# Three one-pass products in place of one wide product in a latent-attention stage, with the softmax division on another engine

## The chip, the cores and the metric

The kernel runs on one core of a Trainium2 chip. A core has five engines with instruction queues of their own: TensorE (PE in the profile; its weight loads stand apart as PEld) multiplies, VectorE (DVE) and ScalarE (ACT) work element by element, GpSimd (POOL) does slower side work, and SyncE (SP) mostly starts DMA transfers. Each engine takes its instructions in a fixed order and waits on semaphores for the others. The metric is the device time of one execution in microseconds (us); lower is better.

## What is computed

The reference is a decoder trunk of two layers on 256 positions of width 2048. Layer A (gated spatial mixing with attention into 256 memory tokens) and both gated feed-forward networks (FFN, with a causal convolution of width 3) are not changed. What matters is layer B, multi-head latent attention with 12 heads:

```python
q = (rmsnorm(q_lat, g_q_lat) @ w_uq).reshape(B, S, 12, 128 + 64)      # q_nope, q_rope
s = (einsum('bqhr,bkr->bhqk', einsum('bqhn,rhn->bqhr', q_nope, w_uk), c_kv)
     + einsum('bqhp,bkp->bhqk', q_rope, k_rope)) * (128 + 64) ** -0.5
p = softmax(where(k_pos <= q_pos, s, -inf))
o = einsum('bqhr,rhv->bqhv', einsum('bhqk,bkr->bqhr', p, c_kv), w_uv)  # 12 heads of 128
x = x + concat([o, memory_attention(q_m)]) @ w_out
x = x + conv_ffn(rmsnorm(x, g_ffn), w_up, cw, cb, w_down)
```

The end is a last rmsnorm. All data are f32.

## The kernel before

**Products in parts.** Activations lie transposed, 128 features by 256 positions in each block. A product with weights (512 KB, four column blocks by two row blocks, in one `chunk`) is made of parts: SP loads `raw` (four buffers), ScalarE rounds it to a high part `whi` in the reduced type fp32r (L110), VectorE subtracts to get the low part `wlo` (L111), four buffers each, and TensorE adds up high x high, high x low and low x high, one pass each. In `mm_fm` that is L147, L148 and L150; `gemm_fm` runs chunks in pairs through it, and its `hooks` are functions called after a numbered chunk. `gemm_tm` and `mm_tm` (L178 to L180) do the same with positions as rows. The activations are split in the same way (`split`, `split_pair`, `split_gain`).

**Small products** of the attention are plain f32, each of which the profile shows as two records. fp32r operands give one record.

**Layer B** first makes the latents `chl` (keys and values) and `qhl` (queries), the rotary key `krs`, already in parts, and the memory queries. Then a loop over six pairs of heads, `i`, runs: `queries(i)` and `keys(i)` (weight products, results copied out of PSUM to `qn` and `kn`); `turn` of the pair `i - 2` (three transposes, copy to `pT`, L889 and L891); in two rounds another third of the value columns by `values`, whose result v lies in the tile `scratch`; `scores` of the pair `i - 1`; `attend` of the pair `i - 2` (L898, L899); and one memory head's scores, turn and output in three successive rounds. Scores are causal: the first 128 queries meet 128 keys, the second 128 queries 256 keys, so a head's content score is one product of 128 moving columns and one of 256 (L865), to which two one-pass rotary products each are added (L867). The value products have the same two widths. In `scores`, VectorE masks and takes the maximum (L872), ScalarE the exponential with its sum (L877), VectorE the reciprocal (L880) and the multiplication by it (L882). The last turns and value products are hooks of the first group of `w_out`.

**Around it.** `w_out` adds to the residual (L554), prepares the FFN's operand (L242, L243) and, on GpSimd, its sum of squares (L268, L273). The FFN starts its first product at once and asks for the root of that sum in a hook: `rstd_bc` adds over the partitions by a product with ones (L262) and computes on VectorE and ScalarE the factors `rb`, first used when the first product's result is taken out (L228). In the last FFN the residual itself is turned from features to positions: four VectorE transposes (`turn` in `run`, L965) and 64 small DMAs on SP (`place`, L972), in hooks of the second and third round, needed when the down projection begins.

**Order.** Outside the first stage the order of each engine is not that of the code: the Tile library orders instructions by a simulated time line, so work that seems ready early can move ahead of code that stands before it, on each engine by itself. Buffers of a tag rotate; a new tile waits until the last reader of the old one is done. There are 8 PSUM banks, all of one tag.

Of the kernel before, what the change touches and what calls it, by code (L numbers as in the profile page):

```python
# [16 lines left out]
P = 128  # L17
# [54 lines left out]
class Kernel:  # L72
# [459 lines left out]
    def memory_turn(self, p, pool, bufs=2):  # L532
        nc = self.nc
        acc = self.psum()
        for mb in range(2):
            for sb in range(2):
                nc.tensor.transpose(
                    acc[:, mb * S + sb * P : mb * S + (sb + 1) * P], p[:, sb, mb * P : (mb + 1) * P], self.ident
                )
        pT = self.tmp(pool, [P, 512], "pT", bufs)  # L540
        nc.scalar.activation(pT, acc, AF.Copy)
        return pT

# [39 lines left out]
    def ffn(self, l, after=None, to_tokens=None, tokens=None):  # L583
        nc, t = self.nc, self.t
        rb = self.tmp(self.cp, [P, S], "rbc", 2)
        xhl, ssum = self.xhl, self.ssum
        first = {1: [lambda: self.rstd_bc(rb, ssum, D)]}
        up, down = t["w_ffn_up"][l], t["w_ffn_down"][l]
        with self.tc.tile_pool(name=self.uid("ff"), bufs=1) as fp:
            g0 = 0  # L590
            for part, ng in enumerate(FF_GROUPS):
                h = self.ap.tile([P, NB, 512], F32R, tag="big", name=self.uid("h"))

                def conv(b, acc):
                    a = self.tmp(fp, [P, 2, S], "a", 2)
                    self.scaled(a, acc, rb)
                    c = self.tmp(fp, [P, 2, S], "c", 3)
                    for i in range(2):
                        w = lambda j: self.cT[:, l, j, b + i : b + i + 1]
                        nc.scalar.activation(c[:, i, :], a[:, i, :], AF.Identity, scale=w(2), bias=w(3))  # L600
                        for j in (1, 0):
                            o = c[:, i, 2 - j :]
                            nc.vector.scalar_tensor_tensor(o, a[:, i, : S - 2 + j], w(j), o, ALU.mult, ALU.add)  # L603
                    return c

                for g in range(g0, g0 + ng):
                    gate = self.tmp(fp, [P, 4, S], "gate", 2)

                    def eg(b, acc):
                        c = conv(4 * g + b, acc)  # L610
                        nc.scalar.activation(gate[:, b : b + 2, :], c, AF.Silu)

                    def ev(b, acc):
                        c = conv(FB + 4 * g + b, acc)
                        hv = self.tmp(fp, [P, 2, S], "hv", 2)
                        nc.vector.tensor_tensor(hv, gate[:, b : b + 2, :], c, ALU.mult)
                        j = 4 * (g - g0) + b
                        self.split_pair(h[:, j : j + 2, :], hv)

                    ks = list(range(NB))  # L620
                    turns = to_tokens[g - 1] if to_tokens is not None and g in (1, 2) else {}
                    self.gemm_fm(self.rows(up, g * 512, 512), ks, 4, lambda k: xhl[:, k, :], eg, hooks=first if g == 0 else {})
                    self.gemm_fm(self.rows(up, FF + g * 512, 512), ks, 4, lambda k: xhl[:, k, :], ev, hooks=turns)
                last = part == len(FF_GROUPS) - 1
                if last and l == 0:
                    self.new_hl()
                dn = down[g0 * 512 : (g0 + ng) * 512]
                for j in range(4):
                    src = self.rows(dn, j * 512, 512)
                    if tokens is not None:  # L630
                        self.gemm_tm(
                            src, 4 * ng, 512, lambda k: h[:, k, :], lambda tb, acc: tokens(j, tb, acc, last), late=3 if last and j == 3 else 0
                        )
                        continue

                    def ed(b, acc):
                        self.add_residual(4 * j + b, acc)
                        if last:
                            after(4 * j + b)

                    self.gemm_fm(src, list(range(4 * ng)), 4, lambda k: h[:, k, :], ed)
                g0 += ng
# [92 lines left out]
    def layer_b(self):  # L735
# [9 lines left out]
        with tc.tile_pool(name="lb", bufs=1) as lb:  # L745
# [32 lines left out]
                return r  # L778

            ek, fk = latent("ck")  # L780
            self.gemm_fm(self.rows(wkv, 0, KR), ks, 4, x, ek, gain=gk, hooks={1: [lambda: self.rstd_bc(rb, ssum, D)]})
            eq, fq = latent("ql")
            self.gemm_fm(self.rows(w, 0, QR), ks, 4, x, eq, gain=gm, hooks={4: [lambda: fk(chl, KR, "g_kv_lat")]})

# [22 lines left out]
            self.gemm_fm(self.rows(w, QR, MW), ks, MH, x, em, gain=gm, hooks=hooks)  # L807

            hl = self.ap.tile([P, NB, 512], F32R, tag="big", name=self.uid("mainhl"))
            scratch = self.ap.tile([P, NB * 512], F32, tag="xhl", name="scratch")  # L810
            v = scratch[:, : 2 * GW].rearrange("p (a c) -> p a c", a=2)
            wuv = t["w_uv"][0].rearrange("r h v -> r (h v)")

            def values(c):
                def ev(tb, acc):
                    nc.scalar.activation(v[:, tb, c * 512 : (c + 1) * 512], acc, AF.Copy)

                self.gemm_tm(self.rows(wuv, c * 512, 512), 4, 512, lambda k: chl[:, k, :], ev)

# [6 lines left out]
            scale = HD ** -0.5  # L826
            qn, qr, kn, pa, pm = {}, {}, {}, {}, {}

            def queries(pr):
                banks = [self.psum() for _ in range(2)]  # L830
                accs = [banks[0][:, :S], banks[0][:, S:], banks[1][:, :S]]
                src = self.rows(wuq, pr * 2 * HD, 2 * HD)
                for c in range(0, 4, 2):
                    hi, lo = self.chunk(src(c, 2), 2, 2 * HD)
                    jobs = []
                    for j, a in enumerate(accs):
                        cols = slice(j * P, (j + 1) * P)
                        jobs += [(a, hi[:, i, cols], lo[:, i, cols], qhl[:, c + i, :], c + i == 0 and j != 1, c + i == 3 and j != 0) for i in range(2)]
                    self.mm_fm(jobs)
                qn[pr] = self.tmp(lp, [P, 2, S], "qn", 2)  # L840
                nc.scalar.activation(qn[pr], banks[0].rearrange("p (j s) -> p j s", j=2), AF.Copy)
                r = rotate(accs[2])
                qr[pr] = self.tmp(lp, [P, 2, S], "qr", 2, F32R)
                for j in range(2):
                    own, far = (slice(o * ROPE, (o + 1) * ROPE) for o in (j, 1 - j))
                    nc.scalar.activation(qr[pr][own, j, :], r[own, :], AF.Copy)
                    tt(qr[pr][far, j, :], r[own, :], qr[pr][own, j, :].bitcast(F32), ALU.subtract)

            def keys(pr):
                kn[pr] = self.tmp(lp, [P, 2, S], "kn", 2)  # L850

                def ev(b, acc):
                    nc.scalar.activation(kn[pr][:, b : b + 2, :], acc, AF.Copy)

                self.gemm_fm(self.rows(wuk, pr * 256, 256), list(range(4)), 2, lambda k: chl[:, k, :], ev, nk=4)

            def scores(h):
# [3 lines left out]
                for qb in range(2):  # L861
                    n = P * (qb + 1)
                    o = sc[:, part[qb]]
                    q = slice(qb * P, (qb + 1) * P)
                    mm(o, qn[pr][:, j, q], kn[pr][:, j, :n], start=True, stop=False)  # L865
                    for i in range(2):
                        mm(o, qr[pr][:, j, q], krs[:, i, :n], start=False, stop=i == 1)  # L867
                mx = self.tmp(lp, [P, 2], "mx", 4)
# [10 lines left out]
                    )  # L879
                nc.vector.reciprocal(den, den)  # L880
                for qb in range(2):
                    nc.vector.tensor_scalar(p[:, part[qb]], p[:, part[qb]], den[:, qb : qb + 1], None, ALU.mult)  # L882
                pa[h] = p

            def turn(h):
                p = pa.pop(h)
                acc = self.psum()
                for i in range(3):
                    nc.tensor.transpose(acc[:, i * P : (i + 1) * P], p[:, i * P : (i + 1) * P], self.ident)  # L889
                pT = self.tmp(lp, [P, 512], "pT", 3)  # L890
                nc.scalar.activation(pT[:, : 3 * P], acc[:, : 3 * P], AF.Copy)  # L891
                pa[h] = pT

            def attend(h):
                pT = pa.pop(h)
                o = self.psum()
                cols = slice(h * P, (h + 1) * P)
                mm(o[:, :S], v[:, 0, cols], pT[:, :S], start=True, stop=False)  # L898
                mm(o[:, P:S], v[:, 1, cols], pT[:, S : S + P], start=False, stop=True)  # L899
                self.split(hl[:, h, :], o[:, :S])  # L900

            def mscores(h):
                pm[h] = self.memory_scores(1, h, qm[:, h, :], lp)

            def mturn(h):
                pm[h] = self.memory_turn(pm[h], lp, 3)

            def mout(h):
                self.memory_out(1, h, pm.pop(h), hl)
# [29 lines left out]
    def run(self):  # L939
# [9 lines left out]
        with tc.tile_pool(name="fin", bufs=1) as fin:  # L949
# [11 lines left out]
            def turn(h):  # L961
                small[h] = self.tmp(fin, [P, 8, 2, 4, 32], "small", 1)
                for j in (0, 4):
                    src = self.x[:, 8 * h + j : 8 * h + j + 4, :].rearrange("p j s -> p (j s)")
                    nc.vector.transpose(small[h][:, j : j + 4].rearrange("p j a b c -> p (j a b c)"), src)  # L965

            def place(h, q):
                lanes = lambda i: slice(32 * i, 32 * i + 32)
# [116 lines left out]
```

## Time and profile before

| | us |
|---|---|
| median of 3 runs (2047.09 to 2047.97) | 2047.1 |
| the profiled execution | 2048.53 |
| its span, first to last instruction | 2046.8 |
| PSUM copies of L841 and L853 (ScalarE, 6 each), mean | 0.585 and 0.589 |
| copy of the turned p, L891 (12), mean | 0.486 |
| copy of the values, L816 (6), mean | 0.595 |
| loads of w_ffn_up, issue to landing, median | 4.2 |

"Busy" counts the time in which an engine has an instruction at work. Matmul records overlap in the pipeline, each longer than its share, so the cost of a product is read from the distance between the starts of successive records in a timeline. A timeline row gives start, duration, engine, line, operation, what is written from what, partitions and elements, and a count of merged records; in square brackets stands the idle time ahead and what ended it. A row of the waits gives the waiting line, what it waited for, the total, the number and the longest. A row of the table by stretches gives the stretch, its length, busy time with instructions of TensorE, its loads, VectorE, ScalarE and GpSimd, then the granted clock, the DMA share and the GB/s.

### The profile page before, as it was taken

How to read it: one execution, taken by the hardware profiler on the slowest of the kernel's cores; microseconds unless marked ns; L12 is line 12 of the kernel's file. 1: busy time of each engine (PE TensorE's matmuls, PEld its weight loads, DVE VectorE, ACT ScalarE, POOL GpSimd, SP SyncE). 2: the span in 40 equal slices, each digit the busy share in tenths (PEclk: the TensorE clock that was granted, in tenths of full speed). 3: DMA queues.
4: the chain of work that ended last, by engine and by line, in shares of the span. 5: the costliest groups of instructions: out<-in, count | busy, mean ns of one | idle time of the engine just before them, and what ended most of it. 6: DMA issues, size and time to landing. Idle time of an engine off the chain costs nothing.

```text
span 2046.8 us, 39055 instructions
## 1 busy us (share of the span) xinstructions
PE 2036.8 (100%) x16232; PEld 1970.7 (96%) x16232; DVE 1356.2 (66%) x1859; ACT 1044.0 (51%) x1345; POOL 94.2 (5%) x125
## 2 busy tenths in 40 slices
PE   9999999999999999999999999999999999999998
PEld 8989999999999999999999999999988999889997
DVE  6855667767556666457688875776655667656665
ACT  6754644555435554345555665455544455434553
POOL 0000013000000000000052001300000000000000
PEclk9999999999999999999999999999999999999999
DMA  8675565666656666566665545786666666666654
GB/s 309 192 225 176 155 197 187 197 196 188 204 187 194 196 194 197 188 196 195 187 196 181 174 129 176 198 224 196 195 195 193 190 198 193 194 195 188 196 185 155
DMA packets 220626, 394.62 MB, mean 193 GB/s; under 512 B 31648, under 2 KB 38176, under 8 KB 220320
## 3 DMA queue, kind: packets, MB, share of 16 engines
q1 hardware_dynamic: 220160, 391.60, 62.0%
q8 instruction: 127, 2.08, 0.4%
q10 hardware_dynamic: 288, 0.52, 0.1%
q14 instruction: 51, 0.42, 0.1%
HBM read 387.88 MB, written 2.10 MB: 191 GB/s over the span
## 4 chain that ended last, share of the span: by engine, by line
PE 99%; POOL 0%; DVE 0%; issue 0%; ACT 0%; POOLq 0%
PE ps L150 26%; PE ps L147 26%; PE ps L148 26%; PE ps L178 6%; PE ps L179 6%; PE ps L180 6%; PE ps L865 0%; PE ps L485 0%; PE ps L484 0%; PE ps L487 0%; PE ps L548 0%; PE ps L513 0%; PE ps L688 0%; PE ps L898 0%; PE ps L867 0%; PE ps L288 0%
## 5 line engine op out<-in xcount | busy, mean ns | idle before, releaser
L111 DVE TENSOR_TENSOR wlo<-raw,whi 128x1024 fp32r<-128x1024 f32 (+1 forms) x672 | 817.5, 1233 | 615.7 <-issue 419.0
L110 ACT ACTIVATE whi<-raw 128x1024 fp32r<-128x1024 f32 (+1 forms) x672 | 705.2, 1056 | 800.3 <-PE ps L148 571.7
L147 PE MATMUL ps<-xhl,whi 128*128 128x256 f32 x3264 | 752.1, 277 | 0.0
L148 PE MATMUL ps<-xhl,whi 128*128 128x256 f32 x3264 | 750.6, 276 | 0.0
L147 PEld LDWEIGHTS ps<-xhl,whi 128*128 128x128 f32 x3264 | 612.8, 188 | 0.3
L148 PEld LDWEIGHTS ps<-xhl,whi 128*128 128x128 f32 x3264 | 612.6, 188 | 0.3
L150 PE MATMUL ps<-xhl,wlo 128*128 128x256 f32 x3264 | 404.3, 276 | 0.0
L150 PEld LDWEIGHTS ps<-xhl,wlo 128*128 128x128 f32 x3264 | 385.6, 188 | 0.2
L147 PE MATMUL ps<-h,whi 128*128 128x256 f32 x704 | 161.6, 276 | 0.0
L148 PE MATMUL ps<-h,whi 128*128 128x256 f32 x704 | 161.5, 276 | 0.0
L603 DVE SCALAR_TENSOR_TENSOR c<-a,cT,c 128x255 f32<-128x255 f32 (+1 forms) x352 | 146.3, 479 | 0.0
L179 PE MATMUL ps<-wlo,h 128*128 128x512 f32 (+1 forms) x364 | 139.0, 382 | 0.0
L180 PE MATMUL ps<-whi,h 128*128 128x512 f32 (+1 forms) x364 | 138.7, 382 | 0.0
L178 PE MATMUL ps<-whi,h 128*128 128x512 f32 (+1 forms) x364 | 138.3, 382 | 0.0
L147 PEld LDWEIGHTS ps<-h,whi 128*128 128x128 f32 x704 | 132.0, 188 | 0.0
L148 PEld LDWEIGHTS ps<-h,whi 128*128 128x128 f32 x704 | 131.9, 188 | 0.0
L600 ACT ACTIVATE c<-a,cT 128x256 f32<-128x256 f32 x176 | 91.6, 591 | 73.9 <-DVE a L228 73.9
L147 PE MATMUL ps<-mainhl,whi 128*128 128x256 f32 x512 | 118.0, 277 | 0.0
L148 PE MATMUL ps<-mainhl,whi 128*128 128x256 f32 x512 | 117.9, 276 | 0.0
L147 PEld LDWEIGHTS ps<-mainhl,whi 128*128 128x128 f32 x512 | 96.1, 188 | 0.0
L148 PEld LDWEIGHTS ps<-mainhl,whi 128*128 128x128 f32 x512 | 96.1, 188 | 0.0
L150 PE MATMUL ps<-h,wlo 128*128 128x256 f32 x704 | 86.9, 276 | 0.0
(246 smaller groups left out, 1973.6 us busy)
## 6 DMA issues: line engine op xcount, KB each, us to landing
raw<-in_w_ffn_up SPq DMA_DIRECT2D x352, 512.0 KB, 4.2
raw<-in_w_ffn_down SPq DMA_DIRECT2D x176, 512.0 KB, 4.7
raw<-in_w_out SPq DMA_DIRECT2D x64, 512.0 KB, 4.8
raw<-in_w_in_a SPq DMA_DIRECT2D x56, 512.0 KB, 4.3
raw<-in_w_mem_kv SPq DMA_DIRECT2D x30, 512.0 KB, 5.2
raw<-in_w_in_b SPq DMA_DIRECT2D x16, 512.0 KB, 3.9
raw<-in_w_uq SPq DMA_DIRECT2D x12, 384.0 KB, 3.2
raw<-in_w_kv_a SPq DMA_DIRECT2D x8, 512.0 KB, 3.8
```

What stands on the lines that cost most here:

```text
L110: nc.scalar.activation(hi[:, :n], raw[:, :n], AF.Copy)
L111: nc.vector.tensor_tensor(lo[:, :n], raw[:, :n], hi[:, :n].bitcast(F32), ALU.subtract)
L147: mm(acc, wh, x[:, :S], start=first, stop=False)
L148: mm(acc, wh, x[:, S:], start=False, stop=False)
L150: mm(acc, wl, x[:, :S], start=False, stop=last)
L178: mm(acc, xh, wh, start=first, stop=False)
L179: mm(acc, xh, wl, start=False, stop=False)
L180: mm(acc, xl, wh, start=False, stop=last)
L600: nc.scalar.activation(c[:, i, :], a[:, i, :], AF.Identity, scale=w(2), bias=w(3))
L603: nc.vector.scalar_tensor_tensor(o, a[:, i, : S - 2 + j], w(j), o, ALU.mult, ALU.add)
```

## The change

- `queries` and `keys` keep high and low parts (`parts`: a copy on ScalarE, a subtraction on VectorE, both out of PSUM) in place of one f32 copy; `values` keeps two halves `vh`, `vl`; the turned p is split too.
- A content score is three one-pass products, high x high, high x low, low x high; so is each value product.
- The division by the softmax sum is a ScalarE copy with a scale.
- To make room: two buffers for the heads' `pT` (of 3), one for the turned memory scores of layer B (of 3 shared ones, under a tag `mT` of its own), and 2048 instead of 4096 bytes of DMA scratch, which lies at address 0 of SBUF, so everything moves by that much.
- `rstd_bc` is called after chunk 3 instead of 1 in both FFNs and at the latent keys.
- The residual's four transposes are pinned: each stays behind the instruction that the code has before it on VectorE.

```diff
-        first = {1: [lambda: self.rstd_bc(rb, ssum, D)]}
+        first = {3: [lambda: self.rstd_bc(rb, ssum, D)]}
...
-            scratch = self.ap.tile([P, NB * 512], F32, tag="xhl", name="scratch")
-            v = scratch[:, : 2 * GW].rearrange("p (a c) -> p a c", a=2)
+            scratch = self.ap.tile([P, NB * 512], F32R, tag="xhl", name="scratch")
+            vh, vl = (scratch[:, o * GW : (o + 2) * GW].rearrange("p (a c) -> p a c", a=2) for o in (0, 2))
...
-                    nc.scalar.activation(v[:, tb, c * 512 : (c + 1) * 512], acc, AF.Copy)
+                    hi, lo = (x[:, tb, c * 512 : (c + 1) * 512] for x in (vh, vl))
+                    nc.scalar.activation(hi, acc, AF.Copy)
+                    tt(lo, acc, hi.bitcast(F32), ALU.subtract)
...
+            def parts(hl, x):
+                nc.scalar.activation(hl[:, 0], x, AF.Copy)
+                tt(hl[:, 1], x, hl[:, 0].bitcast(F32), ALU.subtract)
...
-                qn[pr] = self.tmp(lp, [P, 2, S], "qn", 2)
-                nc.scalar.activation(qn[pr], banks[0].rearrange("p (j s) -> p j s", j=2), AF.Copy)
+                qn[pr] = self.tmp(lp, [P, 2, 2, S], "qn", 2, F32R)
+                parts(qn[pr], banks[0].rearrange("p (j s) -> p j s", j=2))
...
-                    nc.scalar.activation(kn[pr][:, b : b + 2, :], acc, AF.Copy)
+                    parts(kn[pr], acc)
...
-                    mm(o, qn[pr][:, j, q], kn[pr][:, j, :n], start=True, stop=False)
+                    for a, b in ((0, 0), (0, 1), (1, 0)):
+                        mm(o, qn[pr][:, a, j, q], kn[pr][:, b, j, :n], start=a + b == 0, stop=False)
...
-                    nc.vector.tensor_scalar(p[:, part[qb]], p[:, part[qb]], den[:, qb : qb + 1], None, ALU.mult)
+                    nc.scalar.activation(p[:, part[qb]], p[:, part[qb]], AF.Copy, scale=den[:, qb : qb + 1])
...
-                pT = self.tmp(lp, [P, 512], "pT", 3)
-                nc.scalar.activation(pT[:, : 3 * P], acc[:, : 3 * P], AF.Copy)
+                pT = self.tmp(lp, [P, 2, 3 * P], "pT", 2, F32R)
+                parts(pT, acc[:, : 3 * P])
...
-                mm(o[:, :S], v[:, 0, cols], pT[:, :S], start=True, stop=False)
-                mm(o[:, P:S], v[:, 1, cols], pT[:, S : S + P], start=False, stop=True)
+                for kb, q, k in ((0, slice(0, S), slice(0, S)), (1, slice(P, S), slice(S, 3 * P))):
+                    mm(o[:, q], vh[:, kb, cols], pT[:, 0, k], start=kb == 0, stop=False)
+                    mm(o[:, q], vl[:, kb, cols], pT[:, 0, k], start=False, stop=False)
+                    mm(o[:, q], vh[:, kb, cols], pT[:, 1, k], start=False, stop=kb == 1)
...
-                pm[h] = self.memory_turn(pm[h], lp, 3)
+                pm[h] = self.memory_turn(pm[h], lp, 1)
...
-                    nc.vector.transpose(small[h][:, j : j + 4].rearrange("p j a b c -> p (j a b c)"), src)
+                    tc.keep_in_program_order(nc.vector.transpose(small[h][:, j : j + 4].rearrange("p j a b c -> p (j a b c)"), src))
...
-    nc = bacc.Bacc("TRN2", target_bir_lowering=False, num_devices=1, dynamic_dma_scratch_size=4096)
+    nc = bacc.Bacc("TRN2", target_bir_lowering=False, num_devices=1, dynamic_dma_scratch_size=2048)
```

More of the change, by code (lines that the diff above doesn't have):

```diff
@@ L539, in memory_turn @@
                 )
-        pT = self.tmp(pool, [P, 512], "pT", bufs)
+        pT = self.tmp(pool, [P, 512], "mT", bufs)
         nc.scalar.activation(pT, acc, AF.Copy)
@@ L780, in layer_b @@
             ek, fk = latent("ck")
-            self.gemm_fm(self.rows(wkv, 0, KR), ks, 4, x, ek, gain=gk, hooks={1: [lambda: self.rstd_bc(rb, ssum, D)]})
+            self.gemm_fm(self.rows(wkv, 0, KR), ks, 4, x, ek, gain=gk, hooks={3: [lambda: self.rstd_bc(rb, ssum, D)]})
             eq, fq = latent("ql")
@@ L849, in keys @@
             def keys(pr):
-                kn[pr] = self.tmp(lp, [P, 2, S], "kn", 2)
+                kn[pr] = self.tmp(lp, [P, 2, 2, S], "kn", 2, F32R)
                 def ev(b, acc):
-                    nc.scalar.activation(kn[pr][:, b : b + 2, :], acc, AF.Copy)
+                    parts(kn[pr], acc)
                 self.gemm_fm(self.rows(wuk, pr * 256, 256), list(range(4)), 2, lambda k: chl[:, k, :], ev, nk=4)
```

## The prediction

> **What bounds the kernel now.** I read the head of the page first, then the chain of work that ended last, then the list of waits.
>
> ```profile
> span 2046.8 us, 39055 instructions
> PE 2036.8 (100%) x16232; PEld 1970.7 (96%) x16232; DVE 1356.2 (66%) x1859; ACT 1044.0 (51%) x1345; POOL 94.2 (5%) x125
> PE 99%; POOL 0%; DVE 0%; issue 0%; ACT 0%; POOLq 0%
> PE ps L262 <- POOL ssum L273: 1.0, 1, 1.0
> 1327.39 0.28 PE L150 MATMUL ps<-xhl,wlo 128*128 128x256 f32 x1
> 1328.71 0.70 PE L262 MATMUL ps<-ssum,ones 128*128 128x256 f32 x2 [1.04 <-POOL ssum L273]
> ```
>
> TensorE is busy for 2036.8 of 2046.8 us and holds 99% of the chain. Once it has begun it waits a single time: at 1327.39 a product starts, and the next one, the sum of squares of L262, starts 1.32 us later. So two things only can move the time: what TensorE has to do, and whether something new makes it wait. All edits to the arithmetic lie in the heads' stage of layer B, so the next view is the table by stretches.
>
> ```profile
> 1138.00:1242.00 104.00, 104.00 (x771) 98.71 (x770) 78.86 (x216) 71.21 (x159) 0.00 (x0) 1.00 0.44 134
> ```
>
> Of these 104 us TensorE is busy in all, VectorE (third) in 78.9, ScalarE in 71.2. The granted clock is 1.00, so no cold clock can be won back.
>
> **What a product costs.** Records overlap; the cost is the distance between starts. From the timelines of TensorE and of its weight loads:
>
> ```profile
> 1178.68 0.59 PE L898 MATMUL ps<-pT,scratch 128*128 128x256 f32 x2
> 1179.12 0.38 PE L899 MATMUL ps<-pT,scratch 128*128 128x128 f32 x2
> 1179.34 0.60 PE L898 MATMUL ps<-pT,scratch 128*128 128x256 f32 x2
> ...
> 1158.68 1.07 PE L150 MATMUL ps<-chl,wlo 128*128 128x256 f32 x8
> 1159.59 0.60 PE L865 MATMUL ps<-kn,qn 128*128 128x128 f32 x4
> ...
> 1162.45 0.65 PE L865 MATMUL ps<-kn,qn 128*128 128x256 f32 x2
> 1162.74 0.76 PE L867 MATMUL ps<-krs,qr 128*128 128x256 f32 x4
> 1163.34 0.64 PE L865 MATMUL ps<-kn,qn 128*128 128x256 f32 x2
> ...
> 1162.16 0.30 PEld L867 LDWEIGHTS ps<-krs,qr 128*128 128x128 f32 x2
> 1162.39 0.30 PEld L865 LDWEIGHTS ps<-kn,qn 128*128 128x128 f32 x2
> ```
>
> A plain f32 product makes two records: 256 columns take 1179.12 - 1178.68 = 0.44 us, 128 columns take 1179.34 - 1179.12 = 0.22 us, 0.66 us for one head's value products. The content scores have the same two shapes, so I give them the same 0.66.
>
> A one-pass product of 256 columns takes (1159.59 - 1158.68) / 8 = 0.114 us. For 128 columns the key is L867. From 1162.45 to 1163.34 lie one f32 product of 256 columns, two one-pass products of 256 and two of 128: 0.89 - 0.44 - 0.228 = 0.222, so **0.111 us for a one-pass product of 128 columns**, as much as for 256. The loads say why: every product has its own, and the two of L867 and the next are (1162.39 - 1162.16) / 2 = 0.115 us apart. A load takes that long whatever the number of moving columns.
>
> The Trainium skill, page "TensorE: Matmul & The Clock Gate", section "LDWEIGHTS (loading the stationary operand)", has the load's time follow the weights' columns alone, 128 / 1.2 = 107 ns; the rows' 115 ns agree. That rule speaks against this change; with its 107 ns in place of the rows the six products would take 0.66 us, a change of nothing.
>
> **The change part by part.** Everything is set against the profiled execution (2048.53 us, a span of 2046.8 and 1.7 around it) and then carried to the median of 2047.1, 1.4 us lower.
>
> *Scores and values on TensorE.* Per head both lose 0.66 and gain three products of 256 columns and three of 128: 6 x 0.114 = 0.684. 24 times 0.024 is **+0.6 us**. With loads at 0.109 (0.65) it would be -0.2, at the slower pace below +1.4.
>
> ```profile
> 1166.70 0.88 PE L150 MATMUL ps<-qhl,wlo 128*128 128x256 f32 x6
> 1167.42 0.28 PE L147 MATMUL ps<-chl,whi 128*128 128x256 f32 x1
> ```
>
> After the scores at 1163 the plain weight products ran at (1167.42 - 1166.70) / 6 = 0.120 us instead of 0.114: once the loads have lost their lead they stay behind for a while. There will be more loads without cover now, so this can come more often. The stage has 360 query and key products: all of them would be +2.2 us, none 0. I take **+0.3**.
>
> *The wait at 1327.* The hook that asks for the sum of squares goes from chunk 1 to chunk 3, and the residual's transposes leave VectorE's queue there. The 1.32 us become an ordinary 0.11: **-1.2 us**. What is late next would be rb.
>
> ```profile
> 1336.24 0.42 DVE L257 SCALAR_TENSOR_TENSOR rbc<-rbq,rbr 128x256 f32<-128x256 f32 x1
> 1342.35 1.28 DVE L228 TENSOR_TENSOR a<-ps,rbc 128x512 f32<-128x512 f32 x2
> ```
>
> rb is ready at 1336.7; two chunks are 48 products of 0.113, or 5.4 us, so at worst it comes at 1342.1, still ahead of its first use at 1342.35. The same move in layer A and at the latent heads saves nothing, since TensorE does not wait there.
>
> *VectorE and ScalarE in the stage.*
>
> ```profile
> L228 DVE TENSOR_TENSOR qm<-ps,rbc 128x512 f32<-128x512 f32 x2 | 1.3, 684 | 0.0
> L233 DVE TENSOR_TENSOR mainhl<-ps,mainhl 128x256 fp32r<-128x256 f32 x16 | 6.3, 417 | 0.0
> L882 DVE TENSOR_SCALAR p<-p,den 128x256 f32<-128x256 f32 x12 | 4.2, 348 | 0.0
> L882 DVE TENSOR_SCALAR p<-p,den 128x128 f32<-128x128 f32 x12 | 3.4, 285 | 0.3
> L242 ACT ACTIVATE qhl<-ql,gT 128x256 fp32r<-128x256 f32 x4 | 1.7, 501 | 0.0
> L877 ACT ACTIVATE p<-p,mx 128x128 f32<-128x128 f32 x12 | 4.8, 397 | 6.7 <-DVE mx L875 6.7
> ```
>
> New subtractions: 6 for queries, 6 for keys, 6 for values, each 128x512 out of PSUM, 18 x 0.684 = 12.3; 12 of 384 columns, between 0.417 and 0.684, say 0.55: 6.6. Gone: L882, 7.6. VectorE gets +11.3 and stands at 90.2 of 104 us (87%). ScalarE gets 12 x 0.501 + 12 x 0.397 = 10.8 and stands at 82.0 (79%). Both sums stay under TensorE's, which covers them; so far they cost nothing. The division now makes a round trip (ScalarE's exponential, VectorE's reciprocal, ScalarE again); behind it on ScalarE wait the copies that make whi, of which TensorE has four in hand, and the turned p is used a pair of heads later. I take 0.
>
> *Fewer buffers.* pT of the memory heads has one buffer.
>
> ```profile
> 1180.86 0.60 PE L537 MATMUL ps<-ident,mp 128*128 128x128 f32 x4
> 1181.29 1.03 PE L548 MATMUL ps<-pT,mv 128*128 128x256 f32 x4
> ```
>
> ScalarE's copy of the next turn must wait until L548 has read the last one (1182.3 instead of 1181.5): some 0.8 us of ScalarE, three or four times, covered by its 22 us of slack. With two buffers for the heads' pT the earlier pair was read one round before; nothing waits.
>
> *The turned p.* Here the cover is thin.
>
> ```profile
> 1188.97 0.82 PE L889 MATMUL ps<-ident,p 128*128 128x128 f32 x6
> 1191.85 0.59 PE L898 MATMUL ps<-pT,scratch 128*128 128x256 f32 x2
> 1190.61 0.87 ACT L891 ACTIVATE pT<-ps 128x384 f32<-128x384 f32 x2
> 1190.65 0.85 DVE L847 TENSOR_TENSOR qr<-rm,qr 64x256 fp32r<-64x256 f32 x2
> ```
>
> Where no value columns lie between turn and use, the copies ended at 1191.48, 0.37 us ahead of the product. Now a subtraction of 0.55 stands behind each copy, on a VectorE that is occupied to 1191.5: the first low part comes at 1191.5 + 0.55 = 1192.05, 0.2 late. From nothing (another order on VectorE) to 0.2 plus a whole weight subtraction in front (priced among the rivals), I take 0.2 in about three of six pairs: **+0.5 us**.
>
> *The pinned transposes.* Their four instructions and the 64 small transfers on SP move from the output projection into the second and third round of the last FFN.
>
> ```profile
> L965 DVE STREAM_TRANSPOSE small<-xT x4: 1231/1232/1245, 1257.5 to 1325.4; 128x1024 f32<-128x1024 f32 x4
> L972 SPq DMA_DIRECT2D xt<-small  x64: 585/608/1659, 1280.5 to 1355.9; - x64
> ACT whi L110 <- PE ps L148: 571.7, 376, 5.6
> 1343.00:1493.00 150.00, 150.00 (x1326) 150.00 (x1325) 101.68 (x137) 81.96 (x100) 0.00 (x0) 1.00 0.68 204
> ```
>
> VectorE has 48 us free in those 150, ample for 4 x 1.23. On SP 32 transfers take 32 x 0.608 = 19.5 us of a product phase of 21.8 (eight chunks of 24 products at 0.1135, 2.72 each), beside eight weight loads. ScalarE mostly waits for TensorE to free whi (571.7 us), so four raw and four whi tiles are ready: 21.8 us of lead. I take 0.
>
> *The scratch halved* moves addresses. The same weight buffers run at 0.114 and 0.120 in the rows above, so the pace does not hang on the address alone: 0, with the +2.2 above as its end.
>
> **The sum**: +0.6 + 0.3 - 1.2 + 0.5 = +0.2, or 2048.7 for the profiled execution and **2047.3 us** for the median: no change that can be measured (about 0.2%, 4.1 us, is what a measurement of this kernel can tell).
>
> **The rivals.**
> *Columns count, not loads (faster).* If products of 128 columns cost half of 0.114, six take 0.513 instead of 0.66: 24 x 0.147 = -3.5, with the wait -4.7: 2042.4. For it: three passes look cheaper than the wide f32 product (0.342 against 0.44). Against it: the 0.111 of L867. The Trainium skill, "FP8 and Floating Point Precision", section "TensorE Precision Notes", counts four passes for true f32; three instead of four would be a quarter of 24 x 0.66, or -4.0, and 2041.9. The trace agrees for 256 columns only (0.342 is 0.78 of 0.44). Chance 0.08.
>
> *VectorE is late for the turned p (slower).* The mechanism above with a weight subtraction in front:
>
> ```profile
> 1189.40 1.23 DVE L111 TENSOR_TENSOR wlo<-raw,whi 128x1024 fp32r<-128x1024 f32 x1 [0.27 <-ACT whi L110]
> ```
>
> 0.2 + 1.23 = 1.4 us in each of six pairs is 8.6, with the other terms -0.3: 2055.4; at one us a pair 2052.8. It decides from 4.4 / 6 = 0.7 us a pair on. For it: 87% busy and fixed orders. Against it: VectorE also works ahead on weights, so it has room to be reordered, and before no product of the stage waited. Chance 0.13.
>
> *The small transfers starve the last FFN (slower).*
>
> ```profile
> ACT whi L110 <- DMA raw<-in_w_ffn_up: 26.9, 19, 3.8
> ```
>
> If only half of the lead stands when 32 of them come in a row, 19.5 - 10.9 = 8.6 us are lost, perhaps twice: 2055 to 2064. For it: while they ran before, ScalarE did wait for weights, 26.9 us in 19 pieces. Against it: none of that reached TensorE. Chance 0.04.
>
> *The wait stays.* If the sum of squares is still late, 1.2 more: 2048.5, within the forecast.
>
> **How the numbers follow.** No measurable change 0.75 (with the wait that stays and the slow pace in it, 2045 to 2051), faster 0.08, slower 0.13 + 0.04 = 0.17. The forecast's own ends, -1.4 below (loads at 0.109 and no late p) and +3.5 above (slow pace throughout), leave 0.25 outside; the range goes on to 2043.2 towards the first rival and to 2052.0 towards the second, which leaves out the two rivals' far parts, under 0.2.
>
> **What would show it.** Scores and values in the new profile: six one-pass products per head about 0.68 us apart from first to next, products of 128 columns 0.11 apart; at 0.06 the first rival is right. No TensorE wait at L262. VectorE near 90 us in the stage. Idle of TensorE ahead of the value products, released by the low part of pT, would be the second rival; ScalarE waiting for weight transfers and TensorE for wlo in the last FFN, the third. The forecast is wrong if TensorE's busy time leaves 2036.8 by more than 3 us.

## The result and the profile after

The changed kernel takes 2069.2 us (2068.4 to 2070.5, 5 runs) beside 2047.2 of the kernel before (2047.1 to 2048.0): a ratio of 1.0106, 95% interval 1.0092 to 1.0120. It is **slower by 22 us**, above the forecast range. Its profiled execution took 2069.77 us. These are the lines of after that answer to those of before: the head, the busy times, the chain and TensorE's waits.

```profile
span 2068.0 us, 39173 instructions
PE 2047.0 (99%) x16280; PEld 1979.7 (96%) x16280; DVE 1368.3 (66%) x1865; ACT 1051.8 (51%) x1369; POOL 94.4 (5%) x125
PE 95%; SPq 1%; DMA 1%; DVE 1%; ACT 1%; issue 0%; POOLq 0%; POOL 0%; ACTq 0%; DVEq 0%
PE ps L147 <- ACT whi L110: 7.1, 3, 3.7
PE ps L896 <- ACT p L889: 4.5, 3, 2.8
```

Of 21.2 us more span, TensorE's busy time takes 10.2 (the prediction's sign of being wrong was 3), and waits the rest. L262, on which it waited before, is gone from the list, and two new waits stand there: for weights in the last FFN (L147) and for the divided p at the transposes (L896). The chain, 99% TensorE before, now passes through SP's queue and a weight transfer.

To see where the time sits I cut each trace at two starts that all kernels have: the first product of the value columns and the last value product of a head. From the timelines of TensorE, before:

```profile
1139.61 0.40 PE L178 MATMUL ps<-whi,chl 128*128 128x512 f32 x1
1241.91 0.38 PE L899 MATMUL ps<-pT,scratch 128*128 128x128 f32 x2
2038.69 0.28 PE L180 MATMUL ps<-whi,h 128*128 128x256 f32 x1
```

and after:

```profile
1140.11 0.40 PE L178 MATMUL ps<-whi,chl 128*128 128x512 f32 x1
1251.44 0.27 PE L908 MATMUL ps<-pT,scratch 128*128 128x128 f32 x1
2059.87 0.28 PE L180 MATMUL ps<-whi,h 128*128 128x256 f32 x1
```

The heads' stage lies between the first two rows (the second record of L899 starts 0.11 after the row), the rest between the last two. The stage went from 102.4 to 111.3 us, **+8.9**; the rest from 796.7 to 808.4, **+11.8**. The 0.5 us more ahead of the stage are not counted: kernels that change nothing there differ as much (the stage starts at 1139.1 in b_actdiv and at 1140.2 in b_scores).

**The stage.** The first transposes of p, in the loop's third round (they turn the first pair's p; the expectations below call this place the third pair), in TensorE's timeline of after (start, duration, and in brackets the wait):

```profile
1170.58 0.49 PE L896 MATMUL ps<-ident,p 128*128 128x128 f32 x3
1173.87 0.47 PE L896 MATMUL ps<-ident,p 128*128 128x128 f32 x1 [2.80 <-ACT p L889]
1174.00 0.78 PE L178 MATMUL ps<-whi,chl 128*128 128x512 f32 x1
1174.58 0.63 PE L179 MATMUL ps<-wlo,chl 128*128 128x512 f32 x1
```

Three transposes belong to one head, the fourth waits for the next head's p. Then the products of the value columns are 0.58 and 0.42 us apart, where at full clock it is 0.23. The table by stretches says why; all rows are of after, the first over the transposes and most of the wait, the next two behind it; the granted clock is the third number from the end:

```profile
1170.00:1173.00 3.00, 1.07 (x10) 0.83 (x8) 3.00 (x10) 3.00 (x10) 0.00 (x0) 1.00 0.62 167
...
1174.00:1175.50 1.50, 1.50 (x5) 1.21 (x6) 1.44 (x4) 0.94 (x3) 0.00 (x0) 0.50 0.15 49
1175.50:1177.00 1.50, 1.50 (x5) 1.21 (x4) 0.32 (x1) 0.00 (x0) 0.00 (x0) 0.50 0.88 304
```

During the wait VectorE and ScalarE are busy all the time; behind it TensorE's clock is halved until 1177.12. At the loop's end come waits of 0.97 and 0.73 us at L896 and another stretch at half clock. The length of a wait alone does not decide this. In a_nopin (the changed kernel without the pin, below) the same transposes wait the same 2.80 us, and the clock behind it stays at 1.00:

```profile
1173.01 0.33 PE L896 MATMUL ps<-ident,p 128*128 128x128 f32 x1 [2.80 <-ACT p L889]
...
1173.01:1176.40 3.39, 3.39 (x16) 2.80 (x16) 1.89 (x4) 1.33 (x4) 0.00 (x0) 1.00 0.51 158
```

Read in short stretches, the clock of after falls at 1173.70, 1235.14 and 1412.64 and is back after 3.41, 3.41 and 6.83 us. The second and the third fall come 18 and 70 times 3.413 us after the first; in a_dvediv it is 69 and 84 times, in b_pin 16. So what counts here is where a wait lies on a grid of 3.413 us. How much work a step of the grid may hold and still bring the fall is not settled: the step ahead of the first fall holds three transposes and the last products ahead of the wait. The Trainium skill, "TensorE: Matmul & The Clock Gate", section "What's actually happening", has the clock fall back to half after an idle window of some 3.4 us that does not start with the gap; the trace agrees, and the wait of 2.81 us that ends at 1465.38 in the FFN, which lies across a line of this grid (1463.84) and leaves the clock at 1.00, agrees too.

**The last FFN.** SP's queue and ScalarE in after (the count ends a row of SP):

```profile
1384.98 5.22 SPq L101 DMA_DIRECT2D raw<-in_w_ffn_up  x3
1392.12 16.36 SPq L981 DMA_DIRECT2D xt<-small  x24
1408.57 1.06 SPq L101 DMA_DIRECT2D raw<-in_w_ffn_up  x2
1409.68 5.24 SPq L981 DMA_DIRECT2D xt<-small  x8
1415.02 26.40 SPq L101 DMA_DIRECT2D raw<-in_w_ffn_up  x14
```

```profile
1412.60 1.06 ACT L110 ACTIVATE whi<-raw 128x1024 fp32r<-128x1024 f32 x1 [11.13 <-DMA raw<-in_w_ffn_up]
```

```profile
1413.71 0.58 PE L147 MATMUL ps<-xhl,whi 128*128 128x256 f32 x1 [3.69 <-ACT whi L110]
...
1425.93 2.08 PE L150 MATMUL ps<-xhl,wlo 128*128 128x256 f32 x16
...
1465.38 0.38 PE L147 MATMUL ps<-xhl,whi 128*128 128x256 f32 x1 [2.81 <-ACT whi L110]
```

No weight load is issued from 1390.2 to 1408.6, while SP issues 24 small transfers; before, SP put them between the weight loads, at most six in a row. ScalarE finds no weights for 11 us, and TensorE waits 3.7 us, then works at half clock until 1419.5, and stays at the slow pace for long: at 1425.9 sixteen products take (2.08 - 0.28) / 15 = 0.120 us each instead of 0.113. At the second turn 24 small transfers stand in a row again (from 1443.3), and TensorE waits 2.8 us; behind this wait the clock is 1.00 and the pace 0.113.

### The profile page after: what moved, and what is told of

It is laid out like the page before. It is cut to its first block, busy times and chain, and to the rows that moved or that the text cites. A ratio compares the mean times of both kernels' runs of the same rounds, so it can differ in the third digit from the quotient of the medians.

```text
span 2068.0 us, 39173 instructions
## 1 busy us (share of the span) xinstructions
PE 2047.0 (99%) x16280; PEld 1979.7 (96%) x16280; DVE 1368.3 (66%) x1865; ACT 1051.8 (51%) x1369; POOL 94.4 (5%) x125
## 3 DMA queue, kind: packets, MB, share of 16 engines
q8 instruction: 127, 2.08, 0.4%
## 4 chain that ended last, share of the span: by engine, by line
PE 95%; SPq 1%; DMA 1%; DVE 1%; ACT 1%; issue 0%; POOLq 0%; POOL 0%; ACTq 0%; DVEq 0%
PE ps L147 25%; PE ps L148 25%; PE ps L150 25%; PE ps L178 5%; PE ps L180 5%; PE ps L179 5%; SPq L981 1%; DMA raw<-in_w_ffn_up 1%; DMA raw<-in_w_mem_kv 0%; PE ps L548 0%; PE ps L485 0%; PE ps L484 0%; PE ps L487 0%; PE ps L872 0%; PE ps L513 0%
## 5 line engine op out<-in xcount | busy, mean ns | idle before, releaser
L147 PE MATMUL ps<-xhl,whi 128*128 128x256 f32 x3264 | 757.1, 278 | 7.1 <-ACT whi L110 7.1
L147 PEld LDWEIGHTS ps<-xhl,whi 128*128 128x128 f32 x3264 | 614.6, 188 | 8.1 <-ACT whi L110 7.7
L147 PE MATMUL ps<-h,whi 128*128 128x256 f32 x704 | 161.6, 276 | 0.0
L147 PEld LDWEIGHTS ps<-h,whi 128*128 128x128 f32 x704 | 131.9, 188 | 0.0
L147 PE MATMUL ps<-mainhl,whi 128*128 128x256 f32 x512 | 119.4, 278 | 0.0
L147 PEld LDWEIGHTS ps<-mainhl,whi 128*128 128x128 f32 x512 | 97.2, 190 | 0.0
```

The lines of the kernel that those rows point to most:

```text
L147: mm(acc, wh, x[:, :S], start=first, stop=False)
```

## The experiments

My theory after the result: two independent losses, 13 us from the pin and 9 us from p being late. The rivals concern what makes each late. All figures of the stage and the rest come from the same two cuts of each trace; the ratio is to the kernel before, run on the same chip (medians 2047.2 to 2048.2).

| kernel | time, us | ratio (95%) | stage | rest |
|---|---|---|---|---|
| before (profile above) | 2047.2 | | 102.4 | 796.7 |
| changed | 2069.2 | 1.0106 (1.0092 to 1.0120) | 111.3 | 808.4 |
| b_pin | 2061.4 | 1.0065 (1.0050 to 1.0080) | 102.4 | 810.6 |
| b_pin_pool | 2047.7 | 1.0000 (0.9991 to 1.0009) | 102.4 | 795.4 |
| a_nopin | 2055.9 | 1.0036 (1.0023 to 1.0049) | 110.0 | 795.4 |
| a_dvediv | 2066.7 | 1.0091 (1.0076 to 1.0106) | 107.9 | 811.3 |
| b_actdiv | 2048.2 | 1.0001 (0.9991 to 1.0011) | 102.4 | 797.4 |
| b_scores | 2049.8 | 1.0010 (1.0000 to 1.0019) | 104.2 | 796.7 |
| b_values | 2048.5 | 1.0002 (0.9993 to 1.0011) | 102.9 | 796.4 |
| b_cols64 | 2047.8 (1 run) | | 102.9 | 795.9 |
| a_turnlate | 2053.2 | 1.0026 (1.0016 to 1.0036) | 109.0 | 795.4 |
| a_fix | 2049.4 | 1.0006 (0.9997 to 1.0014) | 104.1 | 795.4 |
| b_hook3 | 2047.3 | 0.9998 (0.9989 to 1.0007) | 102.4 | 795.4 |
| b_wide | 2046.5 | 0.9993 (0.9984 to 1.0002) | 101.5 | 795.6 |

**b_pin: the pin alone.**

```diff
-                    nc.vector.transpose(small[h][:, j : j + 4]..., src)
+                    tc.keep_in_program_order(nc.vector.transpose(small[h][:, j : j + 4]..., src))
```

> The kernel before with only the residual's four transposes pinned. Theory: the pin alone makes 24 small transfers stand in one row on SP in the last FFN, the weight loads come 16 us late, TensorE waits some 7.6 us in all, then runs at half clock and at the slower pace; less the 1.2 us of the old wait the time is 2047.2 + 11.7, about 2059. Rival (the FFN's loss needs the changed heads' stage or the moved hook): within 1 us of before, or 1.2 us below it.

It is slower by 13.6 us (11.7 expected), all in the rest (810.6). Its SP queue shows the same picture, and the ratio settles it: the pin needs nothing else of the change to do its harm.

```profile
1382.54 16.88 SPq L972 DMA_DIRECT2D xt<-small  x24
1399.51 1.06 SPq L101 DMA_DIRECT2D raw<-in_w_ffn_up  x2
1400.62 5.20 SPq L972 DMA_DIRECT2D xt<-small  x8
```

**b_pin_pool: the same, the small transfers issued by GpSimd.**

```diff
-                        nc.sync.dma_start(out=out, in_=small[h][lanes(q), :, tb, b, :])
+                        nc.gpsimd.dma_start(out=out, in_=small[h][lanes(q), :, tb, b, :])
```

> The kernel before with the pin, and the 64 small transfers issued by GpSimd instead of SP. Theory (SP's queue is blocked by 24 issues of 0.68 us in a row): the weight loads come in time, TensorE does not wait in the last FFN, 2046 to 2047. Rival (the many small pieces keep the DMA engines or VectorE's transposes keep the weight parts back, whoever issues them): 2055 to 2061, as with the pin alone.

The transfers run at the same place of the FFN, and the loss is gone; the rest is 795.4, 1.3 below before. TensorE does not wait at L262 here, though the hook stands after chunk 1 as before: the pin alone also removes the old wait. ScalarE's wait for these weights, in b_pin and then here:

```profile
ACT whi L110 <- DMA raw<-in_w_ffn_up: 46.6, 21, 11.7
```

```profile
ACT whi L110 <- DMA raw<-in_w_ffn_up: 2.2, 2, 1.2
```

So it was the blocked queue, not the small pieces on the DMA engines nor the transposes on VectorE.

**a_nopin: the change without the pin** (the diff of b_pin, reversed, on the changed kernel).

> The changed kernel without the pin. Theory: the FFN's loss of 12.9 us goes and the heads' stage keeps its 9 us: about 2056.3. Rival (the loss moves elsewhere, since the transposes then meet a busier VectorE): 2060 or more.

2055.9, as the theory has it, with the rest back at 795.4 and the stage still 110.0. The two losses are separate and add up. The stage's waits are those of the changed kernel (2.80, 0.97 and 0.73 us); the 1.3 us less are the half clock that does not follow the first of them. The halved scratch is in this kernel and not in b_hook3, and both have a rest of 795.4, so it costs nothing there.

**a_dvediv and b_actdiv: the division's place**, back on VectorE in the changed kernel, and on ScalarE in the kernel before.

```diff
-                    nc.scalar.activation(p[:, part[qb]], p[:, part[qb]], AF.Copy, scale=den[:, qb : qb + 1])
+                    nc.vector.tensor_scalar(p[:, part[qb]], p[:, part[qb]], den[:, qb : qb + 1], None, ALU.mult)
```

> The changed kernel with the division by the sum back on VectorE. Theory (ScalarE's queue holds the divided p back): the heads' stage loses its waits, 9 us less, about 2060. Rival (VectorE, busy without a gap because of the new subtractions, is what holds p back): VectorE gets 7.6 us more and the stage is as slow or slower, 2068 to 2075.

> The kernel before with only the division moved to ScalarE. Theory (the division's place is the cause): TensorE waits for p in the heads' stage, 3 to 9 us, 2050 to 2056. Rival (the subtractions on VectorE are the cause): VectorE is lighter by 7.6 us, no wait, 2047.

Neither theory held alone. Moved by itself the division costs nothing (1.0001). Taken out of the change it leaves 5.5 of the 8.9 us in the stage: the waits at the loop's end go, that in the third round stays, now for VectorE:

```profile
1173.00 0.48 PE L896 MATMUL ps<-ident,p 128*128 128x128 f32 x1 [2.02 <-DVE p L889]
```

**b_scores and b_values: one kind of product alone** (their lines of the change's diff on the kernel before; b_values with the fewer buffers).

> The kernel before with only the content scores as three one-pass products (parts of queries and keys; division, values and buffers as before). Theory (any of the new subtractions, 0.7 us each in front of the softmax on VectorE, makes p late): the 12 subtractions of queries and keys cost most of it, TensorE waits at the transposes of the third pair, 2050 to 2054. Rival (only all of them together are too much): 2047 to 2048.

> The kernel before with only the value products as three one-pass products (parts of v and of the turned p, with the fewer buffers that go with it). Theory (what is late is p ahead of its transposes, and these subtractions come behind them): 2047 to 2049. Rival (the fewer buffers or the turned p's low part is what is late): 2050 or more, with TensorE's wait at the value products or at the transposes of the memory heads.

The scores alone cost 1.8 us in the stage, of which one wait takes 1.5 (from start to start; the row counts 1.39 of idle time):

```profile
1172.58 0.33 PE L894 MATMUL ps<-ident,p 128*128 128x128 f32 x1 [1.39 <-DVE p L887]
```

Behind it the clock stays at 1.00. The values alone cost 0.5 and make no wait, so neither the fewer buffers nor the turned p's low part is at fault by itself. Together the two cost 5.5 (a_dvediv), more than the 2.3 of their sum: the wait grows from 1.4 to 2.0, gets one of 0.59 in front, and there the half clock follows.

What makes p late begins in VectorE's queue. These stretches of 16 us end at the fourth transpose of after and at the first of before (VectorE is the third busy time):

```profile
1157.87:1173.87 16.00, 13.20 (x112) 12.81 (x111) 15.77 (x43) 12.22 (x31) 0.00 (x0) 0.99 0.55 164
```

```profile
1154.30:1170.30 16.00, 16.00 (x134) 15.74 (x133) 15.44 (x46) 12.44 (x28) 0.00 (x0) 1.00 0.55 169
```

VectorE was full here before the change too: busy for 15.4 of 16 us, and TensorE did not wait. So an instruction that is put in front of p makes p later. VectorE's last longer idle time ends at 1154.86 in after and at 1153.70 in before; from there to the step that prepares the second head's exponential it needs 14.3 us in after and 11.7 in before. Three new subtractions of 0.69 us (L833) lie in between, and a weight subtraction that stood behind that step before. The rows of after, then of before:

```profile
1168.03 1.22 DVE L111 TENSOR_TENSOR wlo<-raw,whi 128x1024 fp32r<-128x1024 f32 x1
1169.16 0.16 DVE L882 TENSOR_SCALAR mx<-mx 128x2 f32<-128x2 f32 x1
```

```profile
1165.42 0.16 DVE L875 TENSOR_SCALAR mx<-mx 128x2 f32<-128x2 f32 x1
...
1166.22 1.22 DVE L111 TENSOR_TENSOR wlo<-raw,whi 128x1024 fp32r<-128x1024 f32 x1
```

b_scores has the order of after (weight subtraction at 1167.44, step at 1168.58), b_values that of before (1165.45, then 1166.39), and only b_scores waits. ScalarE can begin the second head's exponential at 1169.36 only, 3.3 us later than before (1166.10), and in its own fixed order two exponentials of memory heads, a weight copy and two PSUM copies stand between it and the division:

```profile
1173.42 0.80 ACT L889 ACTIVATE p<-p,den 128x128 f32<-128x128 f32 x2
```

**a_turnlate: the value columns ahead of the turn**, without the pin.

```diff
+                if i in (2, 4):
+                    values(i // 2)
                 if i >= 2:
                     turn(2 * i - 4)
                     turn(2 * i - 3)
-                if i in (2, 4):
-                    values(i // 2)
```

> The changed kernel without the pin, with the value columns of rounds 2 and 4 ahead of the turn of p instead of behind it. Theory (p comes some 3 us after TensorE's fixed order asks for it, and nothing else is short): the wait of 3.1 us at the third pair and the half clock behind it, 4.7 us, go; the waits at the end of the loop stay: 2055.9 - 4.7 = 2051. Rival (VectorE is short of time altogether, so the wait turns up at the next place): 2055 or more.

The wait in the third round is gone, but the stage falls by 1.0 us only (109.0 beside 110.0 of a_nopin). The theory counted a half clock there that a_nopin does not have, and the loop's end takes the rest back, with 6.8 us of half clock (3.4 in a_nopin):

```profile
1230.96 1.30 PE L896 MATMUL ps<-ident,p 128*128 128x128 f32 x4 [3.00 <-ACT p L889]
```

Half of the theory failed here: another order helps at the place that it touches, and the end is a second place, where several heads' exponentials and divisions queue on ScalarE.

**a_fix: the division on VectorE, the values ahead, the small transfers on GpSimd, the pin kept.**

> The changed kernel, pin included, with the division back on VectorE, the value columns ahead of the turn, and the 64 small transfers on GpSimd. Theory (three separate waits make up the loss, and the one-pass products themselves cost 0.3 to 0.8 us): no wait of TensorE is left, the heads' stage is 103.0 us against 102.4 before, the rest 1.3 us shorter: 2046.5 to 2047.5, no change. Rival (VectorE short of time altogether with the division on it): a wait of 2 us or more at another place of the stage, 2050 or more.

2049.4, with 0.6 us of wait left at the loop's end and a stage of 104.1, 1.1 above what I expected. That is 20 us better than the change and not distinguishable from before (1.0006, 0.9997 to 1.0014). The three edits together remove nearly all of the loss. Of the stage's 1.7 us above before, the wait takes 0.6, and the products take 0.8 if they cost what they do in b_scores (0.3 beside its wait) and b_values (0.5); some 0.3 us I have not settled.

**b_cols64: fewer columns.** This kernel leaves out the second key block's part of the values' sum for the last 64 queries.

```diff
-                for kb, q, k in ((0, slice(0, S), slice(0, S)), (1, slice(P, S), slice(S, 3 * P))):
+                for kb, q, k in ((0, slice(0, S), slice(0, S)), (1, slice(P, P + 64), slice(S, S + 64))):
```

> The kernel with the value products alone in one-pass form, where the three products of the second key block take 64 moving columns instead of 128 (the values' sum over the second block is left out for the last 64 queries). Theory (weight loads pace products this narrow): the heads' stage stays at 102.9 us within 0.3. Rival (columns pace them): 36 products by 64 columns of 0.44 ns is 1.0 us less, 101.9.

Half the columns in 36 products change nothing: 102.86 us against 102.88 of b_values, both from the unrounded starts. So the columns do not pace products this narrow. That the loads do is not tested apart, but fits the 0.115 us between the loads in the prediction's rows.

**b_hook3: the hook alone.**

> The kernel before with only the sum of squares asked for after chunk 3 instead of 1. Theory: TensorE's wait of 1.2 us ahead of L262 in the last FFN goes and nothing replaces it, 2046.4 to 2046.8 beside 2047.8 of before on this chip. Rival (the late factors delay the first result, and the wait moves there): no change or slower.

The rest is 1.3 us shorter, TensorE no longer waits at L262 and nothing takes its place. The median, 2047.3, lies a little above what I expected, and the timing cannot tell it from before, so this rests on the trace.

**b_wide: one-pass products only where they are wide**, with the hook; the low parts of block 1 are not made. The memory heads have two buffers for their turned scores.

```diff
-                mm(o[:, :S], v[:, 0, cols], pT[:, :S], start=True, stop=False)
-                mm(o[:, P:S], v[:, 1, cols], pT[:, S : S + P], start=False, stop=True)
+                mm(o[:, :S], vh[:, cols], pw[:, 0], start=True, stop=False)
+                mm(o[:, :S], vl[:, cols], pw[:, 0], start=False, stop=False)
+                mm(o[:, :S], vh[:, cols], pw[:, 1], start=False, stop=False)
+                mm(o[:, P:S], v1[:, cols], p1, start=False, stop=True)
```

> The kernel before with the hook after chunk 3, and of the value products only the one of 256 columns as three one-pass products; that of 128 columns stays plain f32. Theory (three one-pass products win 0.10 us at 256 columns and lose 0.12 at 128): 12 x 0.10 = 1.2 us less in the heads' stage, 101.2 us against 102.4, and the 1.3 us of the old wait: 2.5 us below before. Rival (the longer chain from turn to use, a copy, a subtraction and a second copy, makes TensorE wait): 102.4 or more in the stage, the time as with the hook alone.

The stage falls by 0.9 us (1.2 expected), without a wait, and the median is 1.1 us below before, not 2.5: the lowest of all kernels, but 0.9993 with an interval that reaches 1.0002, so the gain rests on the trace too.

## Why the prediction was wrong

**Right.** TensorE bounds the kernel, and the products cost what the rows said. Forecast +0.3 each for scores and values: +0.5 in b_values, and in b_scores 1.8 less a wait of 1.5, which is 0.3. The first rival, columns instead of loads, is refuted by b_cols64. The old wait's 1.2 us came back as 1.3 (b_hook3), and the pin alone brings it as well. The fewer buffers cost nothing by b_values. The +0.3 for more products at the slow pace did not come in the stage: by the distances between starts (0.117 to 0.125 us), 71 weight products run at it before and 28 in after.

**Wrong, the step "VectorE and ScalarE in the stage".** The prediction summed both engines over 104 us, found 87% and 79%, and let TensorE's time cover them. The amounts were about right (over the whole kernel VectorE gained 12.1 us, where 11.3 was forecast, and ScalarE 7.8, where 10.8 was), the cover was not. VectorE's 25 free us lie elsewhere in the stage; in the 16 us ahead of the third round's transposes it was busy for 15.4 before the change, and TensorE's order there was fixed. The new subtractions, and the order of VectorE that came with them, made the second head's exponential 3.3 us later, and TensorE waited 2.8. The same holds for "I take 0" for the division's round trip: 0 by itself (b_actdiv), 3.4 us where the exponentials are already late (111.3 less 107.9).

**Wrong, the step "The turned p".** The second rival looked at the right engine but a step too far on: for 0.2 us at the value products behind the turn. The p was late ahead of the turn, at the transposes, and its price was 2.8 us of waiting at one place and 1.7 at the other, and stretches at half clock of 1.3 us or a little more, which no term of the sum had.

**Wrong, the step "The pinned transposes".** The prediction set 19.5 us of issues against 21.8 us of lead. In the trace SP issues no weight load from 1390.2 to 1408.6, 18.4 us (1.9 idle, then 24 issues); to that come the transfer and the copy until whi is there, to 1413.7, another 5.1, which the prediction left out. The lead was 1409.7 (TensorE's last product ahead of the wait begins) less 1390.2, or 19.5. So 23.5 stood against 19.5, and the 4.0 between them are the wait from start to start. The third rival named the place and had a chance of 0.04; its price of 8.6 per turn was too high for the wait and left out what follows it: of the 13.0 us (11.8 and the old wait's 1.2) the waits of both turns are 7.6 from start to start, and the half clock (2.9) and the slow pace (2.4) make up most of the other 5.4. Why 24 stand in a row is argued and not shown: the planner's simulated time line seems to let the transfers go as soon as their data are there.

**What stays open.** That the waits of scores and values together exceed their sum is put down to VectorE's full queue and, in part, to where the wait lay for the clock; which single subtraction tips it was not tried, nor a kernel with the weight subtraction alone held behind. Some 0.3 us in a_fix are not explained. The upper end of the prediction's own range, +3.5 with the slow pace throughout, comes to 2.9 by its terms (1.4 + 2.2 - 1.2 + 0.5); the result lies far beyond either.

## What to carry to other kernels

A reserve is counted where it is used: take the busy share of the stretch ahead of each fixed point of the bounding engine, not of the stage. Where a helping engine is full there, as VectorE was before the change, look on which side of the late operand the new work stands in its queue: in front it costs its own length, behind it little. An instruction that is pinned or moved takes along every transfer that depends on it; count the issues that may stand in one row on that queue, add the landing and the conversion, and compare with the tiles in hand. And three one-pass products in place of a plain f32 one paid here at 256 moving columns (0.9 us for twelve, in b_wide's stage) and not at 128, so look at the width before the number of passes.

## What the runs showed that I had not expected

The half clock hangs on where a wait lies, not on its length alone: the same wait of 2.80 us brought it in the changed kernel and not in a_nopin, and it is most of the 1.3 us between their stages. So two traces of nearly the same kernel can differ by that much without a difference in any wait of the stage. The slow pace of 0.120 us a product set in behind the half clock at 1419.5 in the changed kernel and held for 356 products, until the next wait at 1462: 2.4 us, summed over the distances between starts. GpSimd issued the 64 transfers of b_pin_pool with no loss elsewhere; its first row there:

```profile
1382.96 8.84 POOL L972 DMA_DIRECT2D xt<-small  x15 [56.86 <-DVE small L965]
```

That is 8.84 / 15 = 0.59 us an issue, about SP's 16.36 / 24 = 0.68 in after.
